# Expert gates of six token tiles: the scattered half made with one-hot products, and a quarter of the one-hots moved to GpSimd

## The chip, the cores and the metric

One core of a Trainium2 chip runs the whole program. The metric is the device time of one execution in microseconds. The engines are named as in the profile: PE is TensorE (PEld its weight loads), DVE is VectorE, ACT is ScalarE, POOL is GpSimd, SP is SyncE, which only issues transfers here. DVE, ACT, POOL and PE each run their own list of instructions strictly in order.

## The reference

Two groups of tokens (256 and 1024) go through one encoder layer with the same weights: a mixer (retention and attention), a memory attention and an expert layer, then a norm. The change is in the expert layer. For each token every one of 8 heads picks 16 experts of 16384 through two lists of 128 keys, so an expert has two indices `i1` and `i2`; the gate `g` is a softmax over the 16.

```python
ids = i1[sel] * 128 + i2[sel]                    # 128 experts a token
g = softmax(ts)                                  # their gates
a = einsum('td,ted->te', xt, U[ids])
out = einsum('te,ted->td', g * gelu(a), V[ids])
```

## The kernel before, in words

The 1280 tokens are ten tiles of 128 (tiles 0 and 1 are the first group). The phases follow each other in program order: `phase_a` (input projections and retention), `phase_b` on tiles 0 and 1 with the attention of the first group ahead of it (`phase_m`), `phase_m` of the second group, `phase_b` on tiles 2 to 5 and then 6 to 9 (the mixer's output, memory attention, and the scores of the expert keys), `gates`, and `dense`.

The expert layer has three parts. *Routing* (`lists`, `pairs`, `route`) is all on DVE: it finds the 16 best keys and pairs of each head and writes the tile's indices and gates. A *gathered* tile (`GATHER`, here 0, 7, 8, 9) then fetches the 128 rows of U and the 128 rows of V that each of its tokens needs: an indirect transfer per row number, issued by POOL (line 1063), and one DVE instruction per fetched row (`gj` for U, `gps` for V). A *dense* tile (here 1 to 6) is multiplied with all experts on PE (`dense`), block by block of 128 experts, and the result is weighted with a gate matrix `gt`, zero for the experts that a token did not pick.

That gate matrix is made in two ways. For tiles 1, 2 and 3 (`SCATTER`) POOL adds the gates into a zeroed array in device memory, `GS`, one indirect transfer for each of the 128 expert numbers of a tile (line 1019, function `scatter`); the arrays are zeroed in `phase_a` (`zeros`). For tiles 4, 5 and 6 (`MADE`) the function `gates` makes it on PE: for each token the one-hot matrix `o1` of its 128 first indices (line 1149 on DVE, or 1157 and 1158 on ACT, for four tokens at a time) and the matrix `o2` of its second indices times the gates (line 1163, DVE) are multiplied into PSUM (1164); ACT copies four tokens' products out (1166), and SP stores 64 tokens at a time in eight pieces (1118). The string `O1_BY` says which engine makes `o1` for which four tokens.

Two things set the order. The class `K` holds lists of generators, `routing`, `gathering` and `scattering`; `tick`, called after each group of matrix products, advances them in proportion to the work just issued (`RHO`, `RHO_S`), so routing, gathering and scattering are woven into the phases. In `gates` only routing is advanced, and none once all dense tiles are routed. What is left of the gathering is issued after `dense` in program order. Then a planner orders each engine's list by simulated time, so such work is moved ahead where the simulation finds room. In the trace, lines 74 and 90 are the helpers `Lead` and `Fill` through which nearly all DVE instructions go: 90 is routing and gathering, 74 the rest.

Of the kernel before, what the change touches and what calls it, by code (L numbers as in the profile page):

```python
# [10 lines left out]
F32 = mybir.dt.float32  # L11
F32R = mybir.dt.float32r
BF = mybir.dt.bfloat16
I32 = mybir.dt.int32
# [7 lines left out]
P = 128  # L22
# [15 lines left out]

GATHER = [0, 7, 8, 9]
DENSE = [t for t in range(NTILE) if t not in GATHER]  # L40
TD = len(DENSE) * P

SCATTER = [1, 2, 3]
MADE = [t for t in DENSE if t not in SCATTER]
TG = 64
HP = PK // 2
NG = 3
O1_BY = ("vaa", "va", "va")

RHO = ((0.75, 0.42), (0.5, 0.0), (0.9, 0.0))  # L50

RHO_S = 0.4
LATE = 2
# [54 lines left out]
class K:  # L108
    def __init__(self, nc, tc, I, O, dbg=None):
        self.nc, self.tc, self.I, self.O = nc, tc, I, O  # L110
        self.dbg = dbg or {}
        self.n = 0
        self.routing, self.gathering, self.scattering = [], [], []
        self.owed_s = 0.0
        self.keeps = []
        self.spare = ()
        self.routed = set()
        self.owed, self.rho = 0.0, (0.0, 0.0)
        self.gps = None
        self.anchor = None  # L120
        self.v, self.vf = Lead(self), Fill(self)

    def tick(self, us):


        self.owed_s = self.owed_s + us * RHO_S if self.scattering and self.rho[0] else 0.0
        while self.owed_s > 0.0 and self.scattering:
            self.owed_s -= self.step(self.scattering)
        rho = self.rho[0 if self.routing else 1]
        if self.rho is RHO[1] and self.routed.issuperset(DENSE):  # L130
            rho = 0.0
        if not (self.routing or self.gathering) or not rho:
            self.owed = 0.0
            return
        self.owed += us * rho
        while self.owed > 0.0 and (self.routing or self.gathering):
            self.owed -= self.step()
# [94 lines left out]
    def setup(self, cp):  # L232
# [8 lines left out]
        for e in (EPS, GEPS):  # L241
            t = cp.tile([P, 1], F32, name=self.nm("eps"))
            self.v.memset(t, e)
            self.eps[e] = t
        self.place = load("place", [P, 1])
        self.normw = load("normw", [P, 4, KC])
# [58 lines left out]
    def phase_a(self, sd):  # L305
# [3 lines left out]
        with ExitStack() as es:  # L309
# [6 lines left out]
            xl = xp.tile([P, KC, T], F32R, name=self.nm("xl"))  # L316
            self.zero = xp.tile([P, 512], F32, name="zero")
            wp = es.enter_context(tc.tile_pool(name="aw", bufs=1, reuse_waits="tile"))
# [12 lines left out]
            with ExitStack() as e2:  # L331
# [5 lines left out]
                def load(t):  # L337
# [7 lines left out]
                    self.transposed(pt, xs, (xh[:, :, sl], xl[:, :, sl]), self.normw[:, 0, :])  # L345
                zeros = self.zeros()
                self.root_table(a0)
                load(0)
                for p in range(RH // 2):
# [9 lines left out]
                    for t in tiles:  # L359
                        if p == 0 and t % 2 == 0 and t + 2 < NTILE:  # L360
                            load(t + 2)
                        if p == 0 and t == 2:
# [3 lines left out]
                            nc.scalar.dma_start(sin, I["sinr"])  # L366
                            nc.gpsimd.memset(self.zero, 0.0)
                        for l, tag in ((vv, "vv"), (gg, "gg")):
# [24 lines left out]
                    for t in tiles:  # L393
                        next(zeros, None)
                        ps = project(ws, t, 256)
# [263 lines left out]
    def phase_b(self, sd, blocks, before=None):  # L659
# [4 lines left out]
        with ExitStack() as es:  # L664
# [74 lines left out]
            for ts in blocks:  # L739
# [96 lines left out]
                with tc.tile_pool(name="brt", bufs=1, reuse_waits="tile") as kp:  # L836
                    for b in range(4):
# [25 lines left out]
                        if b < 3:  # L863
                            self.routing.append(self.lists(sd, order[0], b))
                            if b == 1 and order[0] == MADE[-1]:
                                self.routing.append(self.half(0))
# [95 lines left out]
    def route(self, sd, t, b0):  # L962
# [5 lines left out]
        for b in range(b0, 4):  # L968
            yield from self.lists(sd, t, b)
        yield from self.pairs(slice(PH // 2 if t == MADE[-1] else 0, PH))  # L970
        ts, ii = self.rt[3], self.rt[6]
# [6 lines left out]
        v.tensor_tensor(g, g, sm.unsqueeze(2).broadcast_to([P, PH, TK]), ALU.mult)  # L978
        if t == MADE[-1]:

            self.kept = [ii[:, 0], ii[:, 1], g]
        else:
            nc.sync.dma_start(sd["g"][t], g.rearrange("p h k -> p (h k)"))
# [6 lines left out]
        else:  # L990
            if t in SCATTER:

                row = 2 * P
                v.tensor_scalar(ii[:, 0], ii[:, 0], float(row), self.place, ALU.mult, ALU.add)
                v.scalar_tensor_tensor(ii[:, 0], ii[:, 1], float(PK * row), ii[:, 0], ALU.mult, ALU.add)
                v.tensor_scalar(ii[:, 1], ii[:, 1], float(HP), float(TG - HP * PK * row), ALU.is_ge, ALU.mult)
                ids = ap.tile([P, P], I32, tag="ids", name=self.nm("ids"))
                v.tensor_tensor(ids, ii[:, 0].rearrange("p h k -> p (h k)"), ii[:, 1].rearrange("p h k -> p (h k)"), ALU.add)
                nc.sync.dma_start(sd["ids"][t], ids)
                self.scattering.append(self.scatter(self.gp, sd, t))  # L1000
            elif t != MADE[-1]:
                nc.sync.dma_start(sd["ii"][t], ii.rearrange("p s h k -> p s (h k)"))
        self.routed.add(t)
        yield 0.8


    def scatter(self, gp, sd, t):

        nc, tc = self.nc, self.tc
        ids = gp.tile([P, P], I32, tag="sids", name=self.nm("sids"), bufs=1)  # L1010
        nc.sync.dma_start(ids, sd["ids"][t])
        g = gp.tile([P, P], F32, tag="sg", name=self.nm("sg"), bufs=1)
        nc.sync.dma_start(g, sd["g"][t])
        before = self.zeroed[t]
        for h in range(PH):
            mine = []
            for k in range(TK):
                s = h * TK + k
                r = nc.gpsimd.indirect_dma_start(out=sd["GS"][t].rearrange("l a g h (t o) -> (l a g h t) o", o=1), in_=g[:, s:s + 1], in_offset=None,  # L1019
                                                 out_offset=bass.IndirectOffsetOnAxis(ap=ids[:, s:s + 1], axis=0), compute_op=ALU.add)  # L1020
                for o in mine:
                    tc.declare_no_dep(r.ins, o.ins, reason="other experts")
                for o in before:
                    tc.add_manual_dep(r.ins, o.ins.name, SYNC, reason="the head before")
                mine.append(r)
                yield 1.04
            before = mine
        self.scattered[t] = before

    def zeros(self):  # L1030

        nc = self.nc
        z = self.zero.unsqueeze(1).broadcast_to([P, 4, 512])
        self.zeroed, self.scattered = {t: [] for t in SCATTER}, {}
        for t in SCATTER:
            G = self.sd["GS"][t].rearrange("l a g h t -> (l a g h t)").rearrange("(q p n) -> p q n", p=P, n=512)
            for c in range(0, 32, 4):
                self.zeroed[t].append(self.pace(nc.scalar.dma_start(G[:, c:c + 4], z)))
                yield

# [64 lines left out]
    def gates(self, sd):  # L1105
# [3 lines left out]
        with ExitStack() as es:  # L1109
# [9 lines left out]
            for n, t in enumerate(MADE):  # L1119
                while t not in self.routed:  # L1120
                    self.step()
                if t == MADE[-1]:
                    r = [x.rearrange("p h k -> p (h k)") for x in self.kept]
# [13 lines left out]
                for q in range(P // TG):  # L1137
                    st = ap.tile([P, HP, 2, TG], F32, tag="st", name=self.nm("st"), bufs=2)
                    self.late = self.anchor
                    for k in range(0, TG, 4):  # L1140
# [4 lines left out]
                        c0 = q * TG + k  # L1145
                        by = O1_BY[n]
                        who = by[(c0 // 4) % len(by)]
# [11 lines left out]
                        for j in range(4):  # L1159
                            c = q * TG + k + j  # L1160
                            o1 = o1s[:, j, :]
                            o2 = ap.tile([P, P], F32, tag="o2", name=self.nm("o2"), bufs=12)
                            v.tensor_scalar(o2, io, rT[:, 1, c:c + 1], rT[:, 2, c:c + 1], ALU.is_equal, ALU.mult)
                            nc.tensor.matmul(pt[:, j, :], o1, o2, start=True, stop=True)
# [20 lines left out]
    def dense(self, sd):  # L1185
# [5 lines left out]
        NTG = TD // TG  # L1191
        while self.scattering:
            self.step(self.scattering)
        vb = I["peer_v"].rearrange("(b i) d -> b i d", b=PK)
        with ExitStack() as es:
# [5 lines left out]
            def a_stage(b0):  # L1201
                W, V = [], []
                for n in range(b0, min(b0 + NG, PK)):
                    b = n // 2 + n % 2 * HP
                    if n % 2 == 0:
                        self.gt = ap.tile([P, NTG, 2, TG], F32, tag="gt", name=self.nm("gt"), bufs=2)
                        at = 0
                        for G, last in [(sd["GS"][t], self.scattered[t]) for t in SCATTER] + [(sd["G"], ())]:
                            ng = G.shape[2]
                            r = nc.sync.dma_start(self.gt[:, at:at + ng], G[b])  # L1210
                            for o in last:
                                tc.add_manual_dep(r.ins, o.ins.name, SYNC, reason="scattered")
                            at += ng
                    U = []
# [63 lines left out]
    def run(self):  # L1278
        nc, tc, I = self.nc, self.tc, self.I
        with ExitStack() as es:  # L1280
# [11 lines left out]
            sd["G"] = dp.tile([HP, P, len(MADE) * P // TG, 2, TG], F32, name="G")  # L1292
            sd["GS"] = {t: dp.tile([HP, P, P // TG, 2, TG], F32, name=f"GS{t}") for t in SCATTER}
            self.sd = sd
# [25 lines left out]
def layout(inp):  # L1320
# [42 lines left out]
    A["dpos"] = np.stack([i + 1, P - i, P - 1 - i, i], 1)  # L1363
    i = np.arange(P)
    A["place"] = (i // TG * (2 * TG) + i % TG).astype(np.float32)[:, None]
    A["iota128"] = np.tile(np.arange(P, dtype=np.float32), (P, 1))
# [28 lines left out]
```

## Time and profile before

| | |
|---|---|
| three timed runs | 4538.4, 4547.82, 4554.45 us (median 4547.82) |
| the profiled execution | 4537.65 us, of which the span of the trace is 4535.9 us |
| mean granted TensorE clock | 0.944 of full speed |
| busy: PE, DVE, POOL, ACT | 87%, 68%, 59%, 33% of the span |

From the trace: `phase_a` takes the first 400 us, routing of tiles 0 and 1 runs between 750 and 1010 us, `gates` makes its first `o2` at 1979.6 us and its last at 2206.8 us, and `dense` fills the rest. Busy shares are averages over stages with different limits, so each stage is to be read by itself.

### The profile page before, as it was taken

The numbers are of one execution on the slowest core, as the hardware profiler recorded it, in microseconds if no ns is written. First come the engines' busy times: TensorE is split into PE (matmuls) and PEld (weight loads), VectorE is DVE, ScalarE is ACT, GpSimd is POOL, SyncE is SP. The second block draws the span as 40 slices with busy tenths as digits, with TensorE's granted clock in tenths as the row PEclk, the third lists the DMA queues.
The fourth block names the chain that finished last, engine by engine and source line by source line (L and its number), as shares of the span: only waits on it lengthen the run. The fifth ranks groups of instructions, "written<-read, shape, count | busy, mean of one in ns | idle before, by whom it ended". The sixth has DMA issues, their size and how long they took to land.

```text
span 4535.9 us, 64896 instructions
## 1 busy us (share of the span) xinstructions
PE 3937.6 (87%) x22425; PEld 3477.2 (77%) x22425; DVE 3073.4 (68%) x6808; ACT 1517.1 (33%) x3256; POOL 2677.9 (59%) x2283
## 2 busy tenths in 40 slices
PE   7999988856788989285599999999999999999998
PEld 7999867644577888274577888888888888888887
DVE  5565432844566498176399877777877777777778
ACT  5333544433434343065222222222222222222222
POOL 2230243178666557777436766776767777677775
PEclk9999998988899999698799999999999999999999
DMA  4422577124678867476637888989989989899887
GB/s 147 168 72 87 201 264 276 29 12 87 204 251 264 279 166 193 80 172 124 172 111 239 304 292 304 314 306 308 312 312 310 310 310 309 304 315 310 304 306 262
DMA packets 534843, 1030.49 MB, mean 227 GB/s; under 512 B 100848, under 2 KB 235504, under 8 KB 534512
## 3 DMA queue, kind: packets, MB, share of 16 engines
q0 software_dynamic: 204832, 545.55, 38.4%
q1 hardware_dynamic: 306928, 445.11, 30.0%
q10 hardware_dynamic: 22752, 35.68, 2.2%
q8 instruction: 176, 2.88, 0.3%
q14 instruction: 155, 1.27, 0.1%
HBM read 901.68 MB, written 124.45 MB: 226 GB/s over the span
## 4 chain that ended last, share of the span: by engine, by line
DMA 20%; POOL 14%; issue 11%; DVE 10%; PE 2%; ACT 1%; SPq 0%; POOLq 0%; DVEq 0%; ACTq 0%
DMA grow<-in_peer_v,gids 7%; DMA grow<-in_peer_u,gids 6%; POOL grow L1063 5%; POOL GS L1019 4%; DMA ur<-in_uT 3%; POOL vl L1245 3%; DVE gps L90 3%; POOL ul L1221 2%; DVE dacc L74 1%; DVE gj L90 1%; DVE oh L90 1%; DMA vr<-in_peer_v 1%; DVE wr L74 1%; DVE wl L74 1%; DMA GS<-sg,sids 1%
## 5 line engine op out<-in xcount | busy, mean ns | idle before, releaser
L1019 POOL DMA_INDIRECT GS<-sg,sids x384 | 620.7, 1616 | 314.6 <-DMA sids<-ids 142.7
L90 DVE SCALAR_TENSOR_TENSOR gps<-grow,ga,gps 128x1024 f32<-128x1024 f32 x512 | 657.4, 1284 | 218.4 <-DMA grow<-in_peer_v,gids 210.1
L1063 POOL DMA_INDIRECT grow<-in_peer_u,gids x512 | 529.5, 1034 | 354.1 <-DVE gj L90 222.2
L170 PE MATMUL pa<-dxT,uh 128*128 128x384 f32 x2048 | 690.0, 337 | 15.4 <-ACT uh L1220 12.8
L1063 POOL DMA_INDIRECT grow<-in_peer_v,gids x512 | 510.1, 996 | 321.8 <-DVE gps L90 206.1
L172 PE MATMUL pa<-dxT,ul 128*128 128x384 f32 x2048 | 682.1, 337 | 7.7 <-POOL ul L1221 7.4
L171 PE MATMUL pa<-dxT,uh 128*128 128x384 f32 x2048 | 688.0, 336 | 0.0
L170 PE MATMUL pv<-vh,wh 128*128 128x512 f32 x1536 | 612.0, 401 | 80.1 <-DVE dacc L74 73.4
L171 PE MATMUL pv<-vl,wh 128*128 128x512 f32 x1536 | 615.3, 401 | 20.6 <-POOL vl L1245 20.3
L172 PE MATMUL pv<-vh,wl 128*128 128x512 f32 x1536 | 607.6, 396 | 0.0
L90 DVE SCALAR_TENSOR_TENSOR gj<-grow,gps 128x1024 bf16<-128x1024 f32 x384 | 467.3, 1217 | 185.4 <-DMA grow<-in_peer_u,gids 170.7
L203 POOL TENSOR_TENSOR wl<-wraw,wh 128x512 fp32r<-128x512 f32 x180 | 239.5, 1349 | 342.8 <-ACT wh L199 241.4
L1221 POOL TENSOR_TENSOR ul<-ur,uh 128x512 fp32r<-128x512 f32 x256 | 338.3, 1329 | 148.6 <-ACT uh L1220 141.7
L170 PEld LDWEIGHTS pv<-vh,wh 128*128 128x128 f32 x1536 | 293.0, 191 | 165.2 <-DVE dacc L74 99.9
L170 PEld LDWEIGHTS pa<-dxT,uh 128*128 128x128 f32 x2048 | 386.2, 189 | 29.6 <-ACT uh L1220 17.0
L170 PE MATMUL pj<-act,wh 128*128 128x256 f32 x1088 | 311.6, 295 | 107.0 <-ACT pq L854 88.3
L172 PEld LDWEIGHTS pa<-dxT,ul 128*128 128x128 f32 x2048 | 385.1, 188 | 22.2 <-POOL ul L1221 19.0
L171 PEld LDWEIGHTS pa<-dxT,uh 128*128 128x128 f32 x2048 | 386.3, 189 | 4.2
L171 PEld LDWEIGHTS pv<-vl,wh 128*128 128x128 f32 x1536 | 293.1, 191 | 103.0 <-POOL vl L1245 49.7
L1245 POOL TENSOR_TENSOR vl<-vr,vh 128x512 fp32r<-128x512 f32 x256 | 328.3, 1301 | 68.6 <-ACT vh L1244 55.7
L90 DVE SCALAR_TENSOR_TENSOR gj<-grow,gx 128x1024 bf16<-128x1024 f32 x128 | 191.3, 1494 | 234.3 <-DMA grow<-in_peer_u,gids 233.0
L1220 ACT CAST uh<-ur 128x512 fp32r<-128x512 f32 x256 | 158.7, 621 | 550.0 <-DMA ur<-in_uT 517.9
(287 smaller groups left out, 8761.6 us busy)
## 6 DMA issues: line engine op xcount, KB each, us to landing
ur<-in_uT SPq DMA_DIRECT2D x256, 256.0 KB
vr<-in_peer_v SPq DMA_DIRECT2D x256, 256.0 KB
GS<-zero ACTq DMA_DIRECT2D x24, 1024.0 KB
wraw<-in_peer_wq SPq DMA_DIRECT2D x96, 256.0 KB
G<-st SPq DMA_DIRECT2D x48, 512.0 KB
gt<-GS SPq DMA_DIRECT2D x192, 128.0 KB
gt<-G SPq DMA_DIRECT2D x64, 384.0 KB
wraw<-in_w_out SPq DMA_DIRECT2D x48, 256.0 KB
```

What stands on the lines that cost most here:

```text
L74: r = f(*a, **kw)
L90: r = f(*a, **kw)
L170: mm(ps, a[0], b[0], start=first, stop=False)
L171: mm(ps, a[0], b[1], start=False, stop=False)
L172: mm(ps, a[1], b[0], start=False, stop=last)
L203: (nc.vector if self.spare and k in self.spare else eng).tensor_tensor(wl[:, :n], raw[:, :n], r32(wh[:, :n]), ALU.subtract)
L1019: r = nc.gpsimd.indirect_dma_start(out=sd["GS"][t].rearrange("l a g h (t o) -> (l a g h t) o", o=1), in_=g[:, s:s + 1], in_offset=None, ou ...
L1063: nc.gpsimd.indirect_dma_start(out=u, out_offset=None, in_=src, in_offset=bass.IndirectOffsetOnAxis(ap=ids[:, s:s + 1], axis=0))
L1220: nc.scalar.copy(uh, ur)
L1221: nc.gpsimd.tensor_tensor(ul, ur, r32(uh), ALU.subtract)
L1245: nc.gpsimd.tensor_tensor(vl, vr, r32(vh), ALU.subtract)
```

## The change

- `SCATTER`, `scatter`, `zeros`, the arrays `GS`, the zeroed source tile, the constant `place` and the four index instructions of `route` go.
- `GATHER` becomes 0, 1, 8, 9, and the dense tiles 2 to 7. All six are in `MADE`, so `gates` handles six tiles where it handled three, with 96 stores of 512 KB where there were 48.
- Of each four tokens' `o2`, the last is made by POOL, the others by DVE as before.
- `O1_BY` is "va" for all: the `o1` of four tokens alternately by DVE and ACT (it was one in three by DVE in the first tile).
- The tile whose routing is cut in halves (`HALVED`) is still 6; the one whose indices stay on chip (`KEPT`) is now 7, so tile 6 goes through device memory.
- `dense` loads `gt` with one transfer of 768 KB for two blocks of experts, where it took four.

```diff
-GATHER = [0, 7, 8, 9]
+GATHER = [0, 1, 8, 9]
 DENSE = [t for t in range(NTILE) if t not in GATHER]
-SCATTER = [1, 2, 3]
-MADE = [t for t in DENSE if t not in SCATTER]
+MADE = DENSE
+HALVED, KEPT = [t for t in MADE if t in BLOCKS[-1]][0], MADE[-1]
-O1_BY = ("vaa", "va", "va")
+O1_BY = "va"
...
     def tick(self, us):
-        self.owed_s = self.owed_s + us * RHO_S if self.scattering and self.rho[0] else 0.0
-        while self.owed_s > 0.0 and self.scattering:
-            self.owed_s -= self.step(self.scattering)
...
     route:
-            if t in SCATTER:
...
-                self.scattering.append(self.scatter(self.gp, sd, t))
-            elif t != MADE[-1]:
+            if t != KEPT:
                 nc.sync.dma_start(sd["ii"][t], ii.rearrange("p s h k -> p s (h k)"))
...
     gates:
-                        by = O1_BY[n]
+                        by = O1_BY
...
-                            v.tensor_scalar(o2, io, rT[:, 1, c:c + 1], rT[:, 2, c:c + 1], ALU.is_equal, ALU.mult)
+                            (nc.gpsimd if j == 3 else v).tensor_scalar(o2, io, rT[:, 1, c:c + 1], rT[:, 2, c:c + 1], ALU.is_equal, ALU.mult)
...
     dense:
-        while self.scattering:
-            self.step(self.scattering)
...
-                        for G, last in [(sd["GS"][t], self.scattered[t]) for t in SCATTER] + [(sd["G"], ())]:
...
+                        nc.sync.dma_start(self.gt, sd["G"][b])
```

## Rows read from the trace of the kernel before

**Rows 1.** The page: span; busy tenths of PE in 40 slices of 113 us; the group of the scatters (busy us, mean ns, then idle time of POOL before them and what ended it).

```profile
span 4535.9 us, 64896 instructions
...
PE   7999988856788989285599999999999999999998
...
L1019 POOL DMA_INDIRECT GS<-sg,sids x384 | 620.7, 1616 | 314.6 <-DMA sids<-ids 142.7 <-issue 125.9 <-DMA GS<-sg,sids 45.1
```

**Rows 2.** Busy time by stretch: start and end in us, length, then busy us (instructions) of PE, PEld, DVE, ACT and POOL, the granted clock, the DMA share and GB/s.

```profile
950.00:1200.00 250.00, 146.91 (x789) 103.45 (x788) 104.41 (x201) 78.99 (x148) 198.00 (x134) 0.79 0.46 90
1200.00:1550.00 350.00, 309.21 (x2024) 273.60 (x2023) 219.75 (x402) 141.77 (x322) 216.65 (x171) 0.95 0.80 264
1790.00:1910.00 120.00, 33.61 (x276) 33.21 (x276) 23.41 (x144) 14.32 (x29) 91.01 (x61) 0.67 0.39 66
...
2225.00:2500.00 275.00, 243.91 (x1171) 214.80 (x1170) 251.99 (x814) 75.97 (x135) 128.28 (x101) 0.96 0.58 186
2700.00:4500.00 1800.00, 1721.01 (x8471) 1520.08 (x8470) 1390.70 (x1764) 457.47 (x835) 1271.35 (x1169) 0.99 0.90 308
```

**Rows 3.** Who waited for whom (us in total, times, longest), from four stretches in this order: 940 to 1210, 1210 to 1550, 1780 to 1915 (two rows) and 2100 to 2230 us (three rows).

```profile
DVE gj L90 <- DMA grow<-in_peer_u,gids: 115.3, 19, 50.2
...
DVE gj L90 <- DMA grow<-in_peer_u,gids: 17.1, 7, 7.1
...
DVE gj L90 <- DMA grow<-in_peer_u,gids: 94.2, 3, 93.7
...
PE pj L170 <- ACT pq L854: 86.4, 2, 83.9
...
PE pt L1164 <- ACT st L1166: 86.1, 2, 85.7
ACT uh L1220 <- DMA ur<-in_uT: 85.8, 1, 85.8
```

**Rows 4.** The gathered rows' DVE instructions in 940 to 1210 us, and in 1210 to 1550 us (duration min/median/max in ns, first and last start).

```profile
L90 DVE SCALAR_TENSOR_TENSOR gj<-grow,gx x35: 1203/1225/1292, 1022.2 to 1209.7; 128x1024 bf16<-128x1024 f32 x35
...
L90 DVE SCALAR_TENSOR_TENSOR gj<-grow,gx x81: 1204/1224/6167, 1209.7 to 1540.4; 128x1024 bf16<-128x1024 f32 x81
```

**Rows 5.** POOL in order of time near the end of `gates` (start, duration): two neighbouring scatters, the last one, and the first instruction after it.

```profile
2111.70 1.57 POOL L1019 DMA_INDIRECT GS<-sg,sids  x1 [0.30 <-issue]
2113.57 1.54 POOL L1019 DMA_INDIRECT GS<-sg,sids  x1 [0.30 <-issue]
...
2189.35 1.54 POOL L1019 DMA_INDIRECT GS<-sg,sids  x1 [0.30 <-issue]
2190.36 3.05 POOL L1221 TENSOR_TENSOR ul<-ur,uh 128x512 fp32r<-128x512 f32 x2
```

**Rows 6.** `gates` in steady running, in order of time (start, duration, number merged): DVE (an `o1` of four tokens, eight `o2`, the next `o1`), ACT (from one `o1` to the one two further on), and a run of PE products (two a token).

```profile
2087.03 0.67 DVE L74 TENSOR_TENSOR o<-rT,io 128x512 f32<-128x512 f32 x1
2087.63 2.13 DVE L74 TENSOR_SCALAR o<-io,rT 128x128 f32<-128x128 f32 x8
2089.68 0.68 DVE L74 TENSOR_TENSOR o<-rT,io 128x512 f32<-128x512 f32 x1
...
2088.52 1.29 ACT L1157 ACTIVATE o<-io,nT 128x128 f32<-128x128 f32 x4
2089.70 1.07 ACT L1166 COPY st<-pt 128x512 f32<-128x512 f32 x2
...
2092.35 0.58 ACT L1166 COPY st<-pt 128x512 f32<-128x512 f32 x1
...
2093.34 0.59 ACT L1166 COPY st<-pt 128x512 f32<-128x512 f32 x1
2093.81 1.30 ACT L1157 ACTIVATE o<-io,nT 128x128 f32<-128x128 f32 x4
...
2087.21 3.11 PE L1164 MATMUL pt<-o,o 128*128 128x128 f32 x24 [0.41 <-ACT o L1158]
```

**Rows 7.** DVE time of line 90 (routing alone, in these stretches): tiles 0 and 1 entirely, then what is routed inside `gates`. Last, the `o2` on DVE: duration min/median/max in ns, first and last start in us.

```profile
750.00:1010.00 260.00, 93.05 (x484) 0.88 0.29 65
...
1975.00:2110.00 135.00, 21.17 (x99) 0.92 0.82 187
...
L74 DVE TENSOR_SCALAR o<-io,rT x384: 321/335/655, 1979.6 to 2206.8; 128x128 f32<-128x128 f32 x192
```

**Rows 8.** DVE and POOL on the same on-chip memory. First, durations min/median/max in ns of a DVE product of two 128x128 operands, and of a DVE scaling of 128x1024. Then groups (busy us, mean ns): a DVE scaling of 128x128, and POOL's products of 128x128, of 128x256, and its fill of 128x512.

```profile
L74 DVE TENSOR_TENSOR sw<-pr,sin x80: 277/283/1007, 77.1 to 365.5; 128x128 f32<-128x128 f32 x80
...
L74 DVE TENSOR_SCALAR ld<-ld,rs x24: 701/753/4735, 450.9 to 1773.4; 128x1024 f32<-128x1024 f32 x24
...
L74 DVE TENSOR_SCALAR nT<-rT 128x128 f32<-128x128 f32 x3 | 0.7, 218 | 18.1 <-ACT rT L1133 18.1
...
L373 POOL TENSOR_TENSOR gg<-gg,gw 128x128 f32<-128x128 f32 x40 | 19.5, 492 | 113.5 <-ACT gg L372 113.5
...
L414 POOL TENSOR_TENSOR ks<-qk,dec 128x256 f32<-128x256 f32 x40 | 25.5, 636 | 29.5 <-PE py L434 29.1
...
L367 POOL MEMSET zero<- 128x512 f32 x1 | 0.5, 525 | 0.3 <-POOLq L1381 0.3
```

**Rows 9.** SP's queue inside `gates` (start, us, transfers issued back to back).

```profile
2037.67 30.39 SPq L1118 DMA_DIRECT2D G<-st  x11
...
2075.68 17.95 SPq L1118 DMA_DIRECT2D G<-st  x9
```

More of the change, by code (lines that the diff above doesn't have):

```diff
@@ L47 @@
 NG = 3
-O1_BY = ("vaa", "va", "va")
+O1_BY = "va"
 RHO = ((0.75, 0.42), (0.5, 0.0), (0.9, 0.0))
-RHO_S = 0.4
 LATE = 2
@@ L112, in __init__ @@
         self.n = 0
-        self.routing, self.gathering, self.scattering = [], [], []
-        self.owed_s = 0.0
+        self.routing, self.gathering = [], []
         self.keeps = []
@@ L244, in setup @@
             self.eps[e] = t
-        self.place = load("place", [P, 1])
         self.normw = load("normw", [P, 4, KC])
@@ L316, in phase_a @@
             xl = xp.tile([P, KC, T], F32R, name=self.nm("xl"))
-            self.zero = xp.tile([P, 512], F32, name="zero")
             wp = es.enter_context(tc.tile_pool(name="aw", bufs=1, reuse_waits="tile"))
@@ L345, in load @@
                     self.transposed(pt, xs, (xh[:, :, sl], xl[:, :, sl]), self.normw[:, 0, :])
-                zeros = self.zeros()
                 self.root_table(a0)
@@ L366, in phase_a @@
                             nc.scalar.dma_start(sin, I["sinr"])
-                            nc.gpsimd.memset(self.zero, 0.0)
                         for l, tag in ((vv, "vv"), (gg, "gg")):
@@ L393, in phase_a @@
                     for t in tiles:
-                        next(zeros, None)
                         ps = project(ws, t, 256)
@@ L864, in phase_b @@
                             self.routing.append(self.lists(sd, order[0], b))
-                            if b == 1 and order[0] == MADE[-1]:
+                            if b == 1 and order[0] == HALVED:
                                 self.routing.append(self.half(0))
@@ L969, in route @@
             yield from self.lists(sd, t, b)
-        yield from self.pairs(slice(PH // 2 if t == MADE[-1] else 0, PH))
+        yield from self.pairs(slice(PH // 2 if t == HALVED else 0, PH))
         ts, ii = self.rt[3], self.rt[6]
@@ L978, in route @@
         v.tensor_tensor(g, g, sm.unsqueeze(2).broadcast_to([P, PH, TK]), ALU.mult)
-        if t == MADE[-1]:
+        if t == KEPT:
             self.kept = [ii[:, 0], ii[:, 1], g]
@@ L990, in route @@
         else:
-            if t in SCATTER:
[L993 to L999, printed above, removed]
-                self.scattering.append(self.scatter(self.gp, sd, t))
-            elif t != MADE[-1]:
+            if t != KEPT:
                 nc.sync.dma_start(sd["ii"][t], ii.rearrange("p s h k -> p s (h k)"))
@@ L1004, in route @@
         yield 0.8
[L1007 to L1039, printed above, removed]
     def gather(self, gp, sd, t):
@@ L1121, in gates @@
                     self.step()
-                if t == MADE[-1]:
+                if t == KEPT:
                     r = [x.rearrange("p h k -> p (h k)") for x in self.kept]
@@ L1206, in a_stage @@
                         self.gt = ap.tile([P, NTG, 2, TG], F32, tag="gt", name=self.nm("gt"), bufs=2)
-                        at = 0
-                        for G, last in [(sd["GS"][t], self.scattered[t]) for t in SCATTER] + [(sd["G"], ())]:
[L1209 to L1213, printed above, removed]
+                        nc.sync.dma_start(self.gt, sd["G"][b])
                     U = []
@@ L1292, in run @@
             sd["G"] = dp.tile([HP, P, len(MADE) * P // TG, 2, TG], F32, name="G")
-            sd["GS"] = {t: dp.tile([HP, P, P // TG, 2, TG], F32, name=f"GS{t}") for t in SCATTER}
             self.sd = sd
@@ L1363, in layout @@
     A["dpos"] = np.stack([i + 1, P - i, P - 1 - i, i], 1)
-    i = np.arange(P)
-    A["place"] = (i // TG * (2 * TG) + i % TG).astype(np.float32)[:, None]
     A["iota128"] = np.tile(np.arange(P, dtype=np.float32), (P, 1))
```

## The prediction, made before the changed kernel ran

> **What bounds the kernel now.** I read the page's slices first: PE is busy nine tenths or more nearly everywhere, but falls to 5 or 6 around 1000 us, to 5 around 1850 us and to 2 around 2100 us [rows 1]. From 2700 to 4500 us PE is busy 96% at a granted clock of 0.99 [rows 2], so `dense`, half of the span, is bound by PE, and this change gives PE the same products there: six dense tiles before and after. What can move lies ahead of it.
>
> Then the table by stretch and the waits, for the three holes. In 950 to 1200 us PE is busy 147 of 250 us, POOL 198 [rows 2]; DVE stands 115 us before fetched rows of U, 50 us of it at once [rows 3]. In 1790 to 1910 us PE is busy 34 of 120 us; DVE stands 94 us before one row, and PE waits 86 us behind that [rows 2, 3]. In 2110 to 2196 us nothing runs but POOL's scatters, one each 1.87 us [rows 5]; an ACT cast of the first expert block (`uh`) waits 86 us for a transfer whose buffer POOL has yet to free by a split (`ul`) queued behind the scatters, and ACT's copies of gate products stand behind the cast, so PE waits 86 us too [rows 3, 5]. All three are one thing: POOL's list is in order, and 384 scatters of 1.6 us with gaps between them [rows 1] hold up what DVE or ACT needs next.
>
> That the scatters and not the fetches are late is seen between the holes: in 1210 to 1550 us, with no scatter in POOL's list, 81 rows are consumed with 17 us of waiting, 0.21 us a row [rows 3, 4].
>
> **The change part by part.** *The first hole.* 35 rows fall into it [rows 4]; at 0.21 us they would still cost 7 us, so at most 115 - 7 = 108 us go. From PE's side: 147 us of work at the 88% that it reaches in 1200 to 1550 us (309 of 350) takes 167 us, a gain of 83 us. DVE's wait partly overlaps work that PE still has, so I take PE's number, rounded: **85 us** (75 to 108). *The second hole*: PE's 86 us and DVE's 94 us bound it; **85 us** (80 to 94). *The third*: 86 us both ways; **85 us** (80 to 86), since the cast's buffer is then freed by a split behind short POOL work. Together **-255 us** (-235 to -288).
>
> *The gates.* Six tiles instead of three. In steady running DVE and ACT are both full: DVE spends 0.60 us on an `o1` of four tokens and 2.05 us on eight `o2` (0.256 each), 2.65 us for eight tokens; ACT needs 5.29 us for sixteen tokens (two `o1` and four copies) [rows 6]. DVE's work before: 384 x 0.256 = 98 us, 43 `o1` at 0.60 = 26 us (a third of the first tile's 32 groups, half of the others'), and 21 us of routing [rows 7], together 145 us. The trace has 227 us from first to last `o2` [rows 7], less the 86 us hole 141 us, so the sum is good to 3%.
>
> After: 576 `o2` on DVE are 148 us, 96 `o1` are 58 us. The routing is the 21 us left of tile 6 plus all of tile 7, 93.05 / 2 = 46.5 us [rows 7], which `dense` had: 68 us. That is 274 us without any conflict. ACT: 48 groups of sixteen tokens at 5.29 us, 254 us, below DVE. PE: 24 products in 3.11 us, so 1536 take 199 us. SP: 2.0 to 2.8 us a store [rows 9], 96 stores 191 to 265 us, hidden under DVE; were DVE free of conflicts, SP would be nearly as long, and it would cost what exceeds DVE's time.
>
> *The `o2` on POOL* are 192 instructions of a kind that no row shows. From above, POOL's product of two 128x128 operands takes 492 ns; from below, its fill of 128x512 takes 525 ns, so 128 columns at that rate alone are 131 ns [rows 8]. It reads one operand, so it is nearer the middle: I take 0.33 us. Even at 0.49 us it is 94 us on POOL, no bound by itself. But DVE pays for it: a DVE product of 128x128 takes 283 ns mostly and 1007 ns at worst, 724 ns more, about as long as one of POOL's products of 636 ns that it then meets; a DVE scaling of 128x1024 goes from 753 to 4735 ns [rows 8]. So DVE stands still while POOL works. DVE has no slack in this stage; each POOL `o2` costs it between nothing (POOL slips into gaps) and its whole length. With 0.33 us, 192 cost 63 us; bounds 0 and 94 us. Sum: 274 + 63 = 337 us, against 145 before: **+192 us** (+129 to +223).
>
> A rule of the Trainium skill is about just this: "SBUF — State Buffer", section "Who interferes with whom", says that DVE and GpSimd share one pair of ports as an exclusive lock, that a DVE `tensor_scalar` in its two-port mode and a DVE instruction with two on-chip inputs both take it, and that the loser blocks for the whole instruction. The stretched maxima of [rows 8] agree. By that rule with POOL's 492 ns the stage would take 274 + 94 = 368 us and the kernel 31 us more than I forecast.
>
> What queues behind the new waits: PE's fourth product of each group waits for POOL, then ACT's copy of the group; with twelve buffers of `o2`, three groups deep, that is latency and no rate. Behind POOL's `o2` stand the first splits of `dense`; they cost at most a few of them.
>
> *What `dense` gains.* Tile 7's routing, 46.5 us of DVE, leaves it. In 2225 to 2500 us DVE is busy 252 of 275 us but PE still 244 [rows 2], 89% instead of 96%: 19 us over the stretch, of which a third part (one of three routed tiles) is 6 us. One `gt` transfer in place of four shortens SP's list, which is not the bound. **-5 us** (-46 to 0).
>
> *At nothing*: the zeroing transfers of `phase_a` and their 24 issues on ACT, where PE is busy 9 tenths [rows 1]; the routing order of tiles 0 and 1, both in the same stretch; tile 1 gathered in place of 7, the same 1024 indirect fetches, their pace set by the same calls of `tick`; tile 6's indices through memory, loaded while five tiles ahead of it are made. Their cover is PE's or DVE's own work in the same stretch; without it each would be a few us.
>
> **Sum.** 4535.9 - 255 + 192 - 5 = 4468 us span; the profiled execution is 2 us over its span, 4470 us. The median of the runs shown is 10 us above the profiled execution, so the forecast for a median is **4480 us**, 1.5% faster.
>
> **Rivals.** *POOL hides under DVE.* If the conflict costs next to nothing, DVE takes 274 us and the gates cost +129: 4417 us as a median. For it: beside POOL's scatters, DVE's `o2` keep a median of 335 ns, 14 above their minimum [rows 7]. Against it: the maxima of [rows 8].
>
> *POOL's `o2` is long (the slower side).* A gate instruction with two operations and two per-token operands may cost POOL far more than a product. The gain of 260 us is used up when the gates cost 260 us more, 145 + 260 = 405 us, that is (405 - 274) / 192 = 0.68 us lost per `o2`. From there the kernel is slower; at 0.9 us it takes 4480 + 192 x 0.57 = 4590 us. For it: POOL's products are at 492 ns already with one operation. Against it: they read two operands.
>
> *The holes stay.* The wait of DVE before gathered rows could be that of the fetches themselves, or of other POOL work: then only the third hole goes, 4480 + 170 = 4650 us. Against it: the 0.21 us a row outside the scatters [rows 3, 4].
>
> **How the numbers follow.** The forecast with its bounds (POOL costs DVE 0.15 to 0.5 us each; 4440 to 4515 us) has 0.54. POOL hidden, or `dense` shorter by its whole 46 us, 4400 to 4440 us: 0.22. POOL between 0.5 and 0.8 us, around no change: 0.10. POOL long: 0.09. Holes that stay: 0.05. What a measurement of this kernel can tell from no change is about 0.3%, 14 us: 4534 to 4561 us is "the same". From the 0.10, some 0.06 fall there and 0.03 below it; with a little from either neighbour, faster 0.78, same 0.08, slower 0.14. The range that leaves out no more than 2 in 10 reaches from 4400 to 4550 us.
>
> **What the profile after would show.** No `GS`; no stretch of 50 us with PE idle in 950 to 1200 or around 1800 us, and `gj` waiting 0.2 us a row: the holes right. `o2` from first to last 337 us: 275 us speaks for the hidden rival, over 410 us for the long one, and POOL's mean for the `o2` (0.33 us expected) says which. DVE's `o2` should rise above its median of 335 ns [rows 7] as it stands before POOL. `dense` should keep 96% PE. Most likely to be wrong is the price of POOL's `o2` to DVE, then a planner that moves other work between the gates.

## The result, and the profile after

The changed kernel takes 4413.8 us (median of four runs, 4410.2 to 4415.9), the kernel before on the same chip 4551.1 us: a ratio of 0.970, 95% interval 0.968 to 0.972. That is 3.0% faster; the forecast was 1.5%, 4480 us, with a range from 4400 to 4550 us. The profiled execution took 4415.9 us, of which the span is 4414.1 us. One trace below, that of the experiment "A gate instruction more, in its place", is of an execution of 5468.3 us at a granted TensorE clock of 0.663, so only durations on POOL and DVE are read from it.

The page of the kernel after: span, and busy tenths of PE in 40 slices (of 110 us), to set beside [rows 1].

```profile
span 4414.1 us, 66568 instructions
...
PE   7999888899898999777999999999999999999998
```

The 5 and 6 around 1000 us, the 2 around 1870 us and the two 5s from 2041 to 2268 us are gone (the prediction puts the 2 and a 5 of [rows 1] in each other's place); apart from the first slice the lowest are now three 7s, and they are `gates`. Next come windows over nearly the same work in both kernels. The columns are those of [rows 2]. The first pair of rows runs from 938 us, where 42 and 41 of the 80 exponentials of `phase_m` have started, to the last one (before, then after), the second pair is `dense` from its first product with U to its last (before, then after).

```profile
938.00:1224.60 286.60, 182.64 (x1031) 128.38 (x1029) 132.83 (x263) 101.23 (x191) 213.90 (x145) 0.82 0.46 95
...
2209.20:4495.80 2286.60, 2164.37 (x10623) 1913.25 (x10623) 1800.04 (x2751) 583.79 (x1061) 1536.76 (x1395) 0.99 0.86 293
```

```profile
938.00:1110.10 172.10, 166.88 (x1045) 120.36 (x1043) 132.20 (x270) 103.94 (x196) 41.20 (x37) 1.00 0.48 149
...
1782.00:2069.00 287.00, 221.29 (x1550) 197.85 (x1550) 274.67 (x1036) 262.38 (x683) 213.31 (x195) 0.94 0.69 198
...
2068.90:4374.10 2305.20, 2164.88 (x10615) 1923.37 (x10614) 1771.63 (x2518) 590.08 (x1064) 1529.55 (x1399) 0.98 0.85 292
```

In the first pair POOL's work falls from 214 to 41 us and the stretch from 287 to 172 us. PE, 64% busy before, is 97% busy after. The middle row of after is `gates`: DVE 275 of 287 us, ACT 262, POOL 213. In the last pair PE has the same work, but `dense` is 19 us longer.

The marks below are starts read from the two traces (us), the end apart. Each difference is after less before; "step" is what the stretch since the line above gained or lost.

| mark | before | after | difference | step |
|---|---|---|---|---|
| last exponential of `phase_m` | 1224.6 | 1110.1 | -114 | -114 (hole 1) |
| last residual of `phase_b` | 1761.5 | 1650.1 | -111 | +3 |
| first product of `gates` | 1980.0 | 1784.0 | -196 | -85 (hole 2) |
| last product of `gates` | 2209.1 | 2068.9 | -140 | +56 (hole 3 and gates) |
| last product with U in `dense` | 4495.8 | 4374.1 | -122 | +19 |
| end | 4535.9 | 4414.1 | -122 | 0 |

The first product of `gates` starts anywhere from 1773.3 to 1785.7 us in this trace and seven below, of kernels that differ from this one only from `gates` on; so one trace gives a step ahead of that mark to some 12 us.

Who waited in the kernel after, to set beside [rows 3]: from 700 to 1780 us (us in total, times, longest).

```profile
DVE gj L88 <- DMA grow<-in_peer_u,gids: 17.1, 7, 6.3
```

The same view of before, for 700 to 1980 us:

```profile
DVE gj L90 <- DMA grow<-in_peer_u,gids: 233.0, 30, 93.7
```

The one-hots of `gates` after (duration min/median/max in ns, first and last start), to set beside [rows 7], and the routing in `gates` (DVE alone, line 88):

```profile
L72 DVE TENSOR_SCALAR o<-io,rT x576: 288/336/1301, 1782.6 to 2066.0; 128x128 f32<-128x128 f32 x192
...
L1107 POOL TENSOR_SCALAR o<-io,rT x192: 785/957/2677, 1782.0 to 2066.2; 128x128 f32<-128x128 f32 x192
...
L72 DVE TENSOR_TENSOR o<-rT,io x96: 664/679/737, 1782.0 to 2060.8; 128x512 f32<-128x512 f32 x96
```

```profile
1782.00:2069.00 287.00, 70.05 (x358) 0.94 0.69 198
```

DVE's `o2` last 283 us from first to last, as the rival "POOL hides under DVE" has it (274) and not the forecast (337). But POOL's own `o2` takes 957 ns in the median, where I had taken 330, and where the rival "POOL's `o2` is long" had 900. No price that follows from the length of POOL's instruction fits both readings, so the experiments begin there.

### The profile page after: what moved, and what is told of

It reads as the page before. It is cut to its first block, busy times and chain, and to the rows that moved or that the text cites. A ratio compares the mean times of both kernels' runs of the same rounds, so it can differ in the third digit from the quotient of the medians.

```text
span 4414.1 us, 66568 instructions
## 1 busy us (share of the span) xinstructions
PE 4027.8 (91%) x23202; PEld 3574.7 (81%) x23202; DVE 3159.1 (72%) x7044; ACT 1643.1 (37%) x3570; POOL 2255.5 (51%) x2090
## 3 DMA queue, kind: packets, MB, share of 16 engines
q14 instruction: 155, 1.27, 0.1%
## 5 line engine op out<-in xcount | busy, mean ns | idle before, releaser
L166 PEld LDWEIGHTS pv<-vh,wl 128*128 128x128 f32 x1536 | 294.5, 192 | 58.0 <-DVE wl L72 0.4
L72 DVE TENSOR_TENSOR dacc<-pv,dacc 128x1024 f32<-128x1024 f32 x258 | 311.0, 1218 | 25.8 <-PE pv L166 25.5
```

The source lines that it names most:

```text
L72: r = f(*a, **kw)
L166: mm(ps, a[1], b[0], start=False, stop=last)
```

## The experiments

The first four runs ask what POOL's `o2` costs DVE: next to nothing (theory A of the expectations), or much of its length, or whether DVE was what bounded the gates at all (its rivals).

**All `o2` on DVE.** The changed kernel with one line changed.

```diff
-(nc.gpsimd if j == 3 else v).tensor_scalar(o2, ...)
+v.tensor_scalar(o2, ...)
```

> The changed kernel with all four o2 of a group on DVE, none on POOL. Theory A (POOL's o2 takes 0.96 us, but DVE pays only some 0.09 us for each): DVE alone has 768 x 0.256 + 96 x 0.60 + 70 us of routing = 324 us, so first to last o2 takes 325 to 335 us instead of 284 and the kernel 4455 to 4465 us. Theory B (DVE stands still while POOL works, as forecast): the stage is no longer than with POOL's help, at most 285 us, kernel at most 4415 us. Theory C (ACT, busy 262 of 287 us, bounds the stage): about 290 us, kernel 4415 to 4425 us.

4451.2 us (ratio to before 0.979, 0.976 to 0.981). Its `o2`, and a stretch around its `gates`:

```profile
L72 DVE TENSOR_SCALAR o<-io,rT x768: 299/339/1305, 1784.3 to 2103.2; 128x128 f32<-128x128 f32 x192
...
L72 DVE TENSOR_TENSOR o<-rT,io x96: 665/681/693, 1783.7 to 2098.8; 128x512 f32<-128x512 f32 x96
```

```profile
1780.00:2120.00 340.00, 258.99 (x1644) 227.39 (x1645) 320.71 (x1240) 273.04 (x689) 5.58 (x4) 0.93 0.63 181
```

The `o2` take 319 us, against 283 with a quarter on POOL. So 192 moved instructions save 35 us, 0.18 us each, where DVE spends 0.256 us on one [rows 6]: each of POOL's instructions costs 0.07 us of that again. A holds (319 and 4451 us lie just under its ranges), and its rivals, with at most 290 us, fall. The medians of DVE's instructions look the same in both kernels, 339 and 336 ns for `o2`, 681 and 679 ns for `o1`. The means show where the price lies: first DVE's `o2` in the changed kernel, then here (busy us, mean ns, idle before), then both kernels' `gates` in the columns of [rows 2].

```profile
L72 DVE TENSOR_SCALAR o<-io,rT 128x128 f32<-128x128 f32 x576 | 172.3, 363 | 7.4 <-PE pt L1108 6.7
...
L72 DVE TENSOR_SCALAR o<-io,rT 128x128 f32<-128x128 f32 x768 | 215.7, 341 | 2.7 <-PE pt L1108 2.1
```

```profile
1782.00:2066.30 284.30, 218.59 (x1526) 195.15 (x1526) 271.96 (x1017) 259.68 (x678) 212.64 (x195) 0.94 0.68 197
...
1783.70:2103.50 319.80, 241.24 (x1546) 210.51 (x1546) 315.86 (x1209) 269.00 (x683) 4.29 (x3) 0.93 0.62 177
```

Beside POOL's 192 instructions, 199 of DVE's 576 `o2` last 350 ns or more; without them 5 of 768 do. And DVE is idle for 12 of 284 us, against 4 of 320, so part of the 0.07 us is waiting and not a slower DVE.

**Half of the `o2` on POOL.**

```diff
-(nc.gpsimd if j == 3 else v).tensor_scalar(o2, ...)
+(nc.gpsimd if j % 2 else v).tensor_scalar(o2, ...)
```

> The changed kernel with two of every four o2 on POOL (384 instead of 192). If 0.96 to 1.1 us is what such an instruction needs on POOL, POOL bounds the stage: 384 of them are 367 to 422 us, kernel 4500 to 4550 us. If its length is mostly waiting for DVE and its own time is the shortest seen, 0.785 us: 301 us, kernel about 4430 us. If DVE stood still for each (theory B), DVE's 226 us and POOL's 367 us would add up to some 590 us, kernel over 4700 us.

4485.2 us (0.987, 0.984 to 0.990).

```profile
L1107 POOL TENSOR_SCALAR o<-io,rT x384: 783/842/3077, 1771.5 to 2138.6; 128x128 f32<-128x128 f32 x192
```

```profile
1780.00:2135.00 355.00, 271.48 (x1518) 217.72 (x1516) 244.75 (x808) 264.80 (x663) 354.02 (x374) 0.91 0.53 154
```

POOL is busy in 354 of 355 us: 384 in 367 us, 0.956 us each, is the rate at which it does them beside DVE's `o1`. That is the lower end of the first case expected, and the kernel lies 15 us under its range. DVE now waits for PE, which waits for POOL:

```profile
DVE o L72 <- PE pt L1108: 101.2, 193, 2.7
```

At a quarter POOL needs 192 x 0.956 = 184 us and is busy 213 of 287 us with all its work: it has room, and that is why its length does little harm there.

**A product on POOL beside all `o2` on DVE.** The kernel of the first experiment with 192 products more, of two 128x128 operands, into a tile that nothing reads.

```diff
+if j == 3:
+    jk = ap.tile([P, P], F32, tag="jk", name=self.nm("jk"), bufs=2)
+    nc.gpsimd.tensor_tensor(jk, o2, io, ALU.mult)
```

> All o2 on DVE as in e1_all_dve, and for each group of four tokens POOL multiplies the last o2 with the column numbers into a tile that nobody reads: 192 products of two 128x128 operands more, the kind of the rows from which DVE's price was taken in the forecast. If such a product stops DVE for its length (0.46 to 0.49 us), the stage from first to last o2 grows from 319 us to some 400 us, kernel about 4530 us. If DVE pays no more than for the gate instruction (under 0.09 us), at most 336 us, kernel 4450 to 4470 us.

4473.2 us (0.983, 0.981 to 0.985).

```profile
L1110 POOL TENSOR_TENSOR jk<-o,io x192: 454/459/1963, 1776.3 to 2119.2; 128x128 f32<-128x128 f32 x192
```

The `o2` take 344 us against 319: 25 us for 192 products, 0.13 us of DVE for each 0.46 us of POOL. That is neither the whole length nor nothing; it lies between what was expected. Of DVE's `o2`, 169 of 768 last 450 ns or more.

POOL pays too. Two of its products, then an `o1` of DVE (start, duration):

```profile
1843.42 0.46 POOL L1110 TENSOR_TENSOR jk<-o,io 128x128 f32<-128x128 f32 x1 [1.89 <-DVE o L72]
1844.61 0.77 POOL L1110 TENSOR_TENSOR jk<-o,io 128x128 f32<-128x128 f32 x1 [0.74 <-DVE o L72]
```

```profile
1844.38 0.68 DVE L72 TENSOR_TENSOR o<-rT,io 128x512 f32<-128x512 f32 x1
```

The second product starts while the `o1` runs and lasts 0.31 us longer. So do all of its kind: the 58 that start inside an `o1` take 771 ns in the median, the 132 that meet none 457. In the changed kernel, POOL's `o2` take 1262 ns in the median where they start inside an `o1` (57) and 865 where they meet none (87), so a part of their length is waiting for DVE.

**A gate instruction more, in its place.** As before, but with the instruction of the `o2` itself.

```diff
+    nc.gpsimd.tensor_scalar(jk, o2, rT[:, 1, c:c + 1], rT[:, 2, c:c + 1], ALU.is_equal, ALU.mult)
```

> All o2 on DVE as in e1_all_dve, and for each group of four tokens POOL does one gate instruction more (compare and multiply with two per-token operands, on the last o2) into a tile that nobody reads. If DVE pays 0.02 to 0.09 us for each of the 192, 323 to 336 us from first to last o2, kernel 4455 to 4470 us. If DVE stands still for as long as POOL works (0.8 to 1.0 us), 470 to 510 us, kernel 4600 us or more.

4452.2 us (0.978, 0.977 to 0.980), 1 us from the kernel without the 192 instructions. The durations on POOL and DVE in its trace:

```profile
L72 DVE TENSOR_SCALAR o<-io,rT x768: 289/335/1386, 2223.0 to 2547.2; 128x128 f32<-128x128 f32 x192
...
L1110 POOL TENSOR_SCALAR jk<-o,rT x192: 789/920/2206, 2224.3 to 2547.8; 128x128 f32<-128x128 f32 x192
```

324 us for the `o2`, 5 more than without. So 0.92 us of this instruction costs DVE at most 5 / 192 = 0.03 us, while 0.46 us of a product costs 0.13. The length of a POOL instruction doesn't tell its price to DVE. What differs is that one reads one tensor and the other two; that this is the reason is argued from these two forms only.

The trace of the changed kernel shows both kinds beside each other. Near the end of `gates` three splits of `dense` (`ul`, POOL, two tensors of 128x512) fall in between. DVE's one-hots up to there, then in the ten microseconds that have the splits, and POOL in those ten (start, duration):

```profile
L72 DVE TENSOR_SCALAR o<-io,rT x540: 288/336/464, 1782.6 to 2048.1; 128x128 f32<-128x128 f32 x180
...
L72 DVE TENSOR_SCALAR o<-io,rT x18: 332/344/1301, 2049.8 to 2058.3; 128x128 f32<-128x128 f32 x18
```

```profile
2049.66 2.49 POOL L1157 TENSOR_TENSOR ul<-ur,uh 128x512 fp32r<-128x512 f32 x2
2052.14 4.43 POOL L1107 TENSOR_SCALAR o<-io,rT 128x128 f32<-128x128 f32 x4
2056.55 1.27 POOL L1157 TENSOR_TENSOR ul<-ur,uh 128x512 fp32r<-128x512 f32 x1
```

Beside the first 180 of POOL's `o2`, no `o2` of DVE is longer than 464 ns. The three that last 1224 to 1301 ns start at 2049.8, 2050.9 and 2056.6 us, each with a split of 1.27 us. The same holds with all `o2` on DVE: its three longest, 1.29 to 1.30 us, meet splits too. A maximum is worth nothing until it is known which instruction it met.

**The scatters alone left out of the kernel before.** Tiles 1 to 3 then lack their gates.

```diff
-self.scattering.append(self.scatter(self.gp, sd, t))
+self.scattered[t] = self.zeroed[t]
```

> The kernel before with the 384 scatters left out, all else as it was: the gates of tiles 1, 2 and 3 stay zero, so three tiles lack their experts' part. If the scatters in POOL's list alone make the three holes, 111 + 85 + 86 us go: the kernel takes 4255 to 4275 us, first to last o2 143 us, DVE waits for gathered rows under 30 us ahead of the gates. If the gathered rows are late by themselves, only the third hole goes: 4450 us.

4269.0 us (0.939, 0.936 to 0.942), its span 4264.9 us, 271 us shorter. DVE's wait for the rows of U, in 700 to 1780 us:

```profile
DVE gj L90 <- DMA grow<-in_peer_u,gids: 23.0, 11, 9.1
```

The products of `gates`:

```profile
L1164 PE MATMUL pt<-o,o x768: 274/275/582, 1788.4 to 1931.8; 128*128 128x128 f32 x192
```

The last exponential is at 1111.6 us (1110.1 in the changed kernel), the first gate product at 1788.4 us, and `gates` takes 143 us from first to last product, what the kernel before has without its hole (229 - 86). All three holes were the scatters; the fetches, the other tiles' routing and the zeroing had no part that can be seen. The run takes away POOL's instructions and their transfers together. That it is their place in POOL's list is read from the order there: [rows 5] for the third hole; for the first, 99 scatters that take 162 of the 250 us from 950 to 1200 us; and for the second, the kernel before from 1780 us on, where POOL has nothing but scatters up to these two rows.

```profile
1898.88 1.54 POOL L1019 DMA_INDIRECT GS<-sg,sids  x1 [0.30 <-issue]
1900.73 1.00 POOL L1063 DMA_INDIRECT grow<-in_peer_u,gids  x1 [0.31 <-issue]
```

**Tile 7 gathered and tile 1 dense again.** This puts tile 7's routing back into `dense`.

```diff
-GATHER = [0, 1, 8, 9]
+GATHER = [0, 7, 8, 9]
```

> The changed kernel with the old split of tiles: 0, 7, 8, 9 gathered, 1 to 6 dense, all six through the gates. Tile 7's routing (46 us of DVE) moves from the gates into the dense stage. If DVE bounds the gates, they shrink from 284 us to where ACT takes over, 254 to 262 us; the dense stage then pays 6 us or so if DVE has room there, kernel 4390 to 4400 us. If the dense stage cannot hide that routing, it grows by up to 46 us: kernel 4410 to 4440 us. If the dense stage's 18 us over its length before come from the new split of tiles, they go too: 4375 us.

4423.1 us (0.973, 0.970 to 0.975). Its first and last product with U:

```profile
L164 PE MATMUL pa<-dxT,uh x2048: 331/334/689, 2042.5 to 4379.8; 128*128 128x384 f32 x187
```

Its gates are 262 us from first to last product (285 in the changed kernel), with ACT, 259 of 270 us, the longest engine; its `dense` is 2338 us (2305). So `dense` seemed unable to hide 46 us of routing, which it had hidden before.

**`gt` with four transfers.** The changed kernel, with its transfer of 768 KB cut as it was cut before.

```diff
-nc.sync.dma_start(self.gt, sd["G"][b])
+for at, ng in ((0, 2), (2, 2), (4, 2), (6, 6)):
+    nc.sync.dma_start(self.gt[:, at:at + ng], sd["G"][b][:, at:at + ng])
```

> The changed kernel, but each gt is loaded with four transfers (three of two token groups, one of six) as in the kernel before, from the one array. If the single transfer of 768 KB makes the dense stage 19 us longer than before (first to last product of the first kind 2305 us against 2287 us), it comes back to 2285 to 2292 us, kernel 4393 to 4400 us. If the transfers do not matter and the planner's order does it, 2300 to 2310 us, kernel 4410 to 4420 us.

4390.5 us (0.965, 0.963 to 0.966), 23 us below the changed kernel. First and last product with U:

```profile
L164 PE MATMUL pa<-dxT,uh x2048: 331/334/687, 2062.9 to 4352.2; 128*128 128x384 f32 x187
```

`dense` falls from 2305 to 2290 us, and it begins 6 us earlier. Who waited in `dense`, 2090 to 4350 us, in the changed kernel and then with four transfers:

```profile
DVE wr L72 <- ACT wr L1168: 52.8, 16, 8.0
...
PE pv L164 <- DVE dacc L72: 77.9, 54, 3.5
PE pa L164 <- ACT wr L1168: 32.4, 11, 10.8
```

```profile
DVE wr L72 <- ACT wr L1169: 28.0, 21, 4.7
...
PE pv L164 <- DVE dacc L72: 71.5, 47, 5.3
...
PE pa L164 <- ACT wr L1169: 17.9, 7, 10.8
```

These waits are on the gate product of a block: ACT's gelu out of PSUM (`wr`), DVE's product with `gt`, and PE's next block behind ACT. That the transfers make the difference doesn't rest on one trace: with tile 7 routed in `gates`, `dense` takes 2301 to 2307 us in the five kernels with one transfer (the changed kernel, the first three experiments, five of sixteen) and 2283 and 2290 us in the two with four. Which wait carries it is not shown: in the first and third experiments PE waits only 21 and 19 us behind `wr`, with `dense` at 2307 and 2301 us. The experiment with the other tiles gathered had the single transfer too, so it is repeated below without it.

**Tile 7 gathered, and four transfers.**

> The changed kernel with tiles 0, 7, 8 and 9 gathered (so tile 7's routing falls into dense again) and gt loaded with four transfers. So far dense took 2287 and 2292 us with four transfers and three tiles routed in it, 2290 with four and two tiles, 2305 with one and two, 2338 with one and three. Theory D, the single transfer alone makes dense long, and the more the fuller DVE is: dense returns to 2287 to 2295 us, the gates stay at 262 us, and the kernel takes 4421 - 45 = about 4376 us. Theory E, routing tile 7 costs dense its 32 us whatever the transfers: dense 2338 - 16 = about 2322 us, the kernel about 4405 us, slower than the four transfers alone (4390).

4376.7 us (0.963, 0.961 to 0.965), the lowest median of the kernels that leave nothing out, though its interval overlaps that of both small edits together (0.961 to 0.966, below). First and last product with U, then who waited in its `dense`:

```profile
L164 PE MATMUL pa<-dxT,uh x2048: 331/334/687, 2046.1 to 4338.3; 128*128 128x384 f32 x187
```

```profile
PE pv L164 <- DVE dacc L72: 71.2, 48, 5.1
PE pv L165 <- POOL vl L1182: 20.8, 59, 1.4
PE pa L164 <- ACT wr L1169: 13.0, 4, 11.3
```

`dense` is 2293 us with three tiles routed in it, 2290 with two: theory D holds, and what I had read from the earlier run as the price of tile 7's routing, 32 us, was the single transfer in a `dense` with a fuller DVE. The kernel before and the one without scatters, both with four transfers and three tiles routed, have 2287 and 2292 us. The gates stay at 262 us, so tile 7's routing is better off in `dense`.

**`gt` with two transfers.**

> The changed kernel with gt loaded with two transfers of 384 KB, one for each half of the tokens. The first gate product of a block reads the first half only, so if it is the wait of that product for the whole 768 KB that makes dense long, two transfers give what four give: dense 2288 to 2293 us, the kernel about 4391 us. If it is the number of transfers in flight that matters, two lie between one and four: dense 2295 to 2302 us, the kernel about 4402 us.

4405.1 us (0.968, 0.965 to 0.971), its four runs from 4385.9 to 4408.6, which spans both expectations. In the profiled one, at 4408.2 us, `dense` is 2304 us, as with one transfer, though the wait of PE behind ACT's `wr` is 19.9 us, near that of four. So this trace speaks against the first theory, that what costs is the first gate product's wait for the whole 768 KB; the four times settle neither. Why four transfers are better than one or two stays open.

**Five of sixteen `o2` on POOL**, 240 in place of 192, and then **both small edits together**.

```diff
-(nc.gpsimd if j == 3 else v).tensor_scalar(o2, ...)
+(nc.gpsimd if j == 3 or j == 1 and k % 16 == 0 else v).tensor_scalar(o2, ...)
```

> The changed kernel with five of every sixteen o2 on POOL instead of four (240 in all). DVE saves 48 x 0.256 = 12 us; POOL then has 240 x 0.95 = 228 us and ACT 254 to 262 us, so if DVE bounds the stage, first to last o2 takes 270 to 278 us instead of 284, kernel 4400 to 4408 us. If POOL's uneven share makes PE wait (two of four tokens' o2 on POOL in every fourth group), nothing is gained: 4412 to 4425 us.

4408.8 us (0.969, 0.967 to 0.970).

```profile
L72 DVE TENSOR_SCALAR o<-io,rT x528: 290/336/1133, 1775.3 to 2049.4; 128x128 f32<-128x128 f32 x176
```

> The changed kernel with both small edits: gt loaded with four transfers and five of sixteen o2 on POOL. If the two gains are in separate stages they add: gates 275 us (285 in the changed kernel), dense 2290 us (2305), together 24 us off 4414, so 4390 us; with the medians of the two single edits (23 and 5 us off) 4386 us. If they share a cause (for instance the planner's order of the first dense blocks), the sum is smaller and the time stays near 4391 us of the four transfers alone with dense at 2300 us or more.

4386.2 us (0.964, 0.961 to 0.966). With 240 on POOL alone the `o2` take 274 us, 9 fewer than 283; that is 0.20 us for each `o2` moved. In the medians, 4409 us can't be told from the 4414 us of the changed kernel. With both edits the gates take 277 us and `dense` 2283 us, so in the profiles, one of each, the gains add. In the medians, 4386 us can't be told from the 4390 us of the four transfers alone.

## Why the prediction was right, and where its sum was off

The time lies inside the range and moved the way that was forecast, but below the 4440 to 4515 us that had 0.54; it fell in the 4400 to 4440 us that had 0.22. The holes were right in their cause, the price of POOL's `o2` was wrong by its rule, and other errors partly made up for each other.

- **The holes** (-85, -85, -85). The cause was right: leaving out the scatters alone takes 271 us off the span, inside the bounds of -235 to -288 us. The second and third came out at their size (-85; and `gates` at 143 us without its 86). *The first hole was mis-sized*, -114 us, past DVE's own 108. I had taken PE's 147 us of work at 88%. Over nearly the same work PE was busy 183 us at a granted clock of 0.82 before, and 167 us at 1.00 after, and 97% busy rather than 88%: some 16 us from the clock and 167 / 0.88 - 172 = 18 us from the share. The 88% was read in a stretch with other waits, and PE's work was counted in microseconds at the lower clock, which it had in a stretch where it was idle 40% of the time [rows 2].
- **The gates without conflict** (274 us). The measured 283 us with POOL's part and 319 us without it (by the same rows 274 + 192 x 0.256 = 323) bear the sum out to 3%; routing was 70 us for my 68.
- **POOL's `o2`, and its price to DVE** (+63 us). This is the step that failed. Its length was 0.957 us in the median, not 0.33, and its price 0.05 us (283 - 274 over 192) to 0.07 us (the first experiment), not 0.33. The two errors run against each other: with the true length and my rule "DVE stands still while POOL works", the gates would have taken 274 + 184 = 458 us, and the kernel would have been slower. The rule came from maxima [rows 8] whose company I had not looked up: the trace of before has the product of 1007 ns beside a weight split on POOL of 0.93 us, not beside a product of 636 ns, and the scaling of 4735 ns beside four such splits of 4.91 us together. They are products of two tensors, another form than the `o2`. The better hint was in [rows 7], 335 ns beside POOL's scatters, which I gave to the rival. It is a median, though, and hides a price: the 312 `o2` that meet a scatter take 368 ns in the mean, the other 72 take 338.
- **The rule of the Trainium skill** ("SBUF — State Buffer", section "Who interferes with whom"): the loser blocks for the whole instruction. The `o2` of 1.3 us beside splits of 1.27 us agree, and so do POOL's instructions that start inside an `o1` and last 0.3 to 0.4 us longer in the median. DVE beside POOL's gate instruction doesn't: no `o2` is longer than 464 ns beside 180 of them, and the 34 `o1`, instructions with two on-chip inputs, that start while one runs take 679 ns in the median, as the others do. The measurement decides; the stage takes 283 us, not my 368 us by that rule.
- **`dense`** (-5 us, measured +19). The part on routing was right: with four transfers 2290 us with two tiles routed in it, 2293 with three. The part on `gt` was wrong. I wrote that one transfer "shortens SP's list, which is not the bound" and priced it at nothing; it cost 15 us in `dense` (2305 against 2290) and 23 us in the medians. That the list is not the bound was no reason for nothing; by which path the transfer costs is not shown.
- **Sum.** In the span, holes -285 (114 + 85 + 86), gates +142, `dense` +19, and 3 us between the first two holes: -121, against -68. 29 of the 53 us come from the first hole, 50 from the gates, and 24 went the other way in `dense`. The terms put at nothing were not run one by one. The likeliest case was not what happened: the kernel lies at the 4417 us of the rival "POOL hides under DVE", with a larger first hole and a longer `dense` that nearly cancel, which is luck.

## What to carry to other kernels

Before pricing contention by the longest duration of an instruction, find which instruction of the other engine it overlapped, and price each form by itself: here one form of POOL cost DVE 0.03 to 0.07 us for 0.96 us of work, another (a split of 128x512) its whole length. Compare means and not medians when a part of the instructions may be slowed. A hole can be worth more than its idle time when PE's clock falls in it, so take the work from a stretch at full clock. Cutting or merging a transfer is not free because its queue has room: it is to be measured by itself.

## What the runs showed of the hardware

- POOL's instruction with a comparison and a product by two per-token operands takes 783 ns at least and some 956 ns in a row on 128x128, about twice its product of two tensors (454 ns at least, 459 median). It costs DVE 0.03 to 0.07 us, the product 0.13 us, so it is the cheaper of the two to run beside DVE's one-hots.
- Either of them lasts longer when it starts inside DVE's one-hot with two on-chip inputs (128x512): 771 ns against 457 for the product, 1262 against 865 for the other.
- DVE's one-hot of 128x128 beside a POOL split of 128x512 takes 1224 to 1301 ns, the length of the split (1262 to 1267 ns).
- 64 transfers of 768 KB in place of 256 smaller ones of the same bytes made a PE-bound stage 15 us longer (2305 against 2290; 2301 to 2307 in five kernels against 2283 and 2290), and 45 us longer (2338 against 2293) where DVE had 46 us of routing in it too.
